# Attention's transposes and the previous step's products with the values in one burst per step, ordered by weight columns

## The chip, the cores and the metric

The kernel runs on one core of a Trainium2 chip. The metric is the device time of one execution in microseconds; three timed runs of the kernel before gave 1712.32, 1714.13 and 1714.29, so its median is 1714.13 us. The profile is one further execution of the same program, which took 1711.05 us.

## What is computed

One decoder block on 1024 tokens of width 1024 in float32: a pre-norm and one wide projection, then dilated sliding-window attention (24 heads in three groups) beside a causal convolution module, a gated merge, and a feed-forward part. The change touches the attention only. Of the reference, cut to what matters:

```python
qb = to_sub(q, 0).reshape(B, dilation, nb, BLOCK, H, Dh)       # queries, 128 a block
kb, vb = band(k), band(v)                                       # their keys and values
s = jnp.einsum('brnqhd,brnkhd->brnhqk', qb, kb) * (Dh ** -0.5) + bias
s = jnp.where(valid[:, None], s, NEG_INF)
lse = jax.nn.logsumexp(s, axis=-1)
p = jnp.exp(s - lse[..., None])
o = jnp.einsum('brnhqk,brnkhd->brnqhd', p, vb)
...
alpha = jax.nn.softmax(jnp.stack(lses, axis=0), axis=0)
o = jnp.einsum('gbsh,gbshd->bshd', alpha, jnp.stack(outs, axis=0))
```

## The kernel before, in words

Nearly all of the kernel is matrix products on TensorE. Every float32 operand is held as a rounded part "hi" and a rest "lo", and a product is three matmuls (hi by hi, hi by lo, lo by hi).

**Where attention lies.** Its work is not a stage of its own. `attention` (line 974) is a generator, and `beat` (line 139) advances it: each matmul of the loops that call `beat` adds RATE to a credit, and for each whole credit the generator runs to its next `yield`. Two loops carry it. The first is the projection of the values, `v` (lines 948, 950 and 952: 128x256 matmuls, called V matmuls below), at RV = 0.42. The second is the products of the convolution's output projection, `unit` (lines 305, 307 and 309: 128x512), at RU = 0.8. The emission order is the execution order: each engine takes its instructions one after the other, and an instruction that waits for another engine holds up what stands behind it on its own.

**One step.** There are 96 block-and-head-pair units in 12 stacks of 8 (group g, head pair hp, query block u) and 101 steps, because step s works on several units at once:

- `att_s` for unit s: four score matmuls (line 1049; 128 or 256 columns), two reductions on VectorE (line 1052) which add the bias and take the row's extremum. `att_e` for unit s-1: two exponentials on ScalarE with their accumulator reads (line 1062). Then a `yield`.
- `att_t` for unit s-4 (LT = 4): two to four 128x128 transposes through the identity (line 1087) into one PSUM bank. ScalarE copies the bank to hi (line 1094), VectorE makes lo from the bank and hi (line 1095). Then a `yield`.
- `att_p` for unit s-5 (LP = 5): the products with the values (line 1122), whose weights are 66 columns of the values and whose moving operand is hi or lo. In groups 0 and 1 there are three with 256 moving columns (called wide below), then three or six with 128 (slim); in group 2 six slim ones. After each of the first two triples there is a `yield`. For every second unit VectorE then copies the result out (line 1142, two copies).

So a step has four yields, and at 0.42 a yield is followed by two or three V matmuls; a step spans 9.5 of them. hi, lo, the scores' tiles and the bias tiles come from one ring of 11 half-size buffers (`half`). Loads of queries, keys and values are issued from SP's queue at the step's start, their doubling (lines 886, 887) and the splitting of the values (lines 917, 918, 922) go to POOL and ScalarE, and POOL's queue also issues the store of a finished stack (line 1149).

**Other work between.** Splits of weights for coming products (lines 188, 189), splits of the convolution's activations (lines 1242, 1243), and the merge of the three groups (lines 1170 to 1188; its one transpose is line 1183) are issued between the matmuls by `tick`.

Of the kernel before, what the change touches and what calls it, by code (L numbers as in the profile page):

```python
# [10 lines left out]
F32R = mybir.dt.float32r  # L11
AF = mybir.ActivationFunctionType
OP = mybir.AluOpType
# [16 lines left out]
ROOT = 1 / 32  # L30
LN_EPS = 1e-5

RV, RU = 0.42, 0.8


LD, PC = 2, (18, 20, 26)
# [22 lines left out]
def f(ap):  # L59
    return ap.bitcast(F32)  # L60


class Build:
# [909 lines left out]

    def attention(self):

        live, s, total = {}, 0, 96
        order = [(g, 2 * hg + i) for hg in range(2) for g in range(3) for i in range(2)]
        nxt, cur, u, x, V = self.stacks(*order.pop(0)), None, 8, None, None
        for i in range(5):
            self.stack_load(nxt)  # L980
        second = self.stacks(*order.pop(0))

        def there():
            return nxt[1] // 2 * 3 + nxt[0] < self.vn

        while s < total + self.LP:
            if s < total:
                if x is None and nxt and there():
                    x = self.values(*nxt[:2])
                if u == 8:  # L990
                    while self.normed < 9 or x is None:
                        if second and second[5] < min(5, self.normed - 4):
                            self.stack_load(second)
                        if x is None and there():
                            x = self.values(*nxt[:2])
                        yield 0
                    if cur is None:
                        self.double(nxt, 0)
                        self.double(nxt, 1)
                    cur, u, nxt, V = nxt, 0, None, []  # L1000
# [12 lines left out]
                if u in (6, 7) and nxt:  # L1013
                    self.double(nxt, u - 6)
                if u == 8:
                    cur[2] = cur[3] = V = None
                if u == 1:
                    if second:
                        nxt, second = second, None
                    elif order:  # L1020
                        nxt = self.stacks(*order.pop(0))
                if nxt and nxt[5] < 5:
                    self.stack_load(nxt)
            if 0 <= s - 1 < total:
                self.att_e(live[s - 1])
            yield 0
            if 0 <= s - self.LT < total:
                self.att_t(live, s - self.LT)
                yield 0
            if 0 <= s - self.LP < total:  # L1030
                yield from self.att_p(live, s - self.LP)
            s += 1

    def att_s(self, a, p, V, u):
# [41 lines left out]
    def att_t(self, live, k):  # L1076


        nc = self.nc
        a, b, hh = live[k & ~1], live[k | 1], k & 1  # L1080
        u = a["u"]
        items = [(a, u), (b, u), (a, u - 1), (b, u + 1)]
        items = [(x, x["blocks"].index(kb)) for x, kb in items if kb in x["blocks"]]
        ps = self.bank("t")
        for j, (x, i) in enumerate(items):
            c = hh * 256 + i * 128
            nc.tensor.transpose(ps[:, j * 128:(j + 1) * 128], x["sp"][:, c:c + 128], self.ident)  # L1087
        x = None
        if hh:
            a["sp"] = b["sp"] = None  # L1090
        n = len(items) * 128
        items = None
        hi, lo = self.half(F32R), self.half(F32R)
        nc.scalar.copy(hi[:, :n], ps[:, :n])
        nc.vector.tensor_tensor(lo[:, :n], ps[:, :n], f(hi[:, :n]), op=OP.subtract)
        a["pt", hh] = hi, lo

    def att_p(self, live, k):


        nc = self.nc
        a, b, hh = live[k & ~1], live[k | 1], k & 1
        g, hp, u = a["g"], a["hp"], a["u"]
        if hh == 0:
            a["o"] = self.bank("o")
        ps = a["o"]
        hi, lo = a.pop(("pt", hh))

        if g == 2:
            todo = [(u, 0, 128, 0), (u + 1, 128, 128, 128)]  # L1110
        else:
            n = 256 + 128 * (len(a["blocks"]) > 1)
            todo = [(u, 0, 256, 0)] + [(u - 1, 256, 128, 0)] * (n > 256) + [(u + 1, n, 128, 128)]
        for j, (kb, x, n, q) in enumerate(todo):
            kb = self.place(g, kb)
            v, w = a["V"][kb // 4]
            c = (kb % 4) * 256 + hh * 128
            vh = v[:, c:c + 66]
            vl = v[:, c + 64:c + 130] if c < 896 else w
            o = ps[0:66, hh * 256 + q:hh * 256 + q + n]  # L1120
            for i, (y, z) in enumerate(((vh, hi), (vl, hi), (vh, lo))):
                nc.tensor.matmul(o, y, z[:, x:x + n], start=i == 0 and j == 0, stop=i == 2 and j == len(todo) - 1,  # L1122
                                 skip_group_check=True)
            if j < 2:
                yield 0
        hi = lo = v = w = vh = vl = y = z = None
        if hh == 0:
            return
        if u == 0:
            self.O = self.ring()  # L1130

        O = self.O
        e = (8, 2, 128)[g]
        if g == 0:
            d = O.rearrange("p (c m) -> p m c", c=8)[:, u * 16:u * 16 + 32]
        elif g == 1:
            d = O.rearrange("p (e c m) -> p c m e", e=2, c=4)[:, u // 2]
        else:
            d = O[:, u * 128:u * 128 + 256].rearrange("p (c m) -> p c m", c=2)
        for h in range(2):  # L1140
            x = ps[0:64, h * 256:(h + 1) * 256]
            nc.vector.tensor_copy(d[h * 64:(h + 1) * 64], x.rearrange("p (a e) -> p a e", e=e))
        a["o"] = ps = d = x = O = None
        del live[k - 1], live[k]
        if u == 6:

            kept = g == 2 and hp > 1
            if not kept:
                self.later(1, lambda x=self.O: nc.gpsimd.dma_start(self.d_att[g, hp], x))
            if g == 2:  # L1150
                self.merges.append(self.bg(self.merge(hp, a["p"][4], self.O if kept else None)))
            self.O = None
# [882 lines left out]
```

## Time and profile before

| what | value |
|---|---|
| median of three runs | 1714.13 us |
| the profiled execution | 1711.05 us |
| span of its instructions | 1709.1 us |
| TensorE clock granted | 0.999 of full |
| first score matmul to last product with values | 614.9 to 862.7 us |
| of these, beside the V matmuls | to 793 us |
| products with values (line 1122) | 648, of them 192 wide |
| transposes (line 1087) | 280 |
| score matmuls (line 1049) | 384 |

The profile names instructions by engine and source line: PE is TensorE's matmuls, PEld its weight loads, DVE is VectorE, ACT is ScalarE, POOL is GpSimd. Matmuls overlap: each row's duration is latency too, so what a matmul costs is read from the distance between the starts of consecutive rows, not from its own duration. A row of the timeline that ends in "x3" is three instructions in a run, its time from the first start to the last end.

### The profile page before, as it was taken

To read this page: it belongs to the slowest core of one execution; us is meant where nothing else is said; L and a number is where in the kernel's file an instruction comes from. 1 tells how busy PE (TensorE), PEld (TensorE's weight loads), DVE (VectorE), ACT (ScalarE), POOL (GpSimd) and SP (SyncE) were. 2 spreads that over 40 slices of the span, in tenths; PEclk is the share of its full clock that TensorE was granted. 3 is DMA by queue.
4 is the path that set the end of the run, shared out by engine and by line. 5 is a ranking of instruction groups with operands and counts; after the bars stand their busy time and mean duration, and the time that the engine had idled before them with its cause. 6 is when DMAs were issued, how large, how long until landed. Compare 5 with 4: busy or idle time off the path is not lost.

```text
span 1709.1 us, 24547 instructions
## 1 busy us (share of the span) xinstructions
PE 1692.4 (99%) x8758; PEld 1437.4 (84%) x8758; DVE 1251.2 (73%) x2214; ACT 790.1 (46%) x1550; POOL 474.5 (28%) x383
## 2 busy tenths in 40 slices
PE   8999999999999999999999999999999999999998
PEld 7788888888888999999878888888888888888886
DVE  6789988888998667677885855775566556677686
ACT  6344344434444576677722436633333333354463
POOL 0017777887886124544300210000000000000000
PEclk9999999999999999999999999999999999999999
DMA  4352433455668887878998722123222322494234
GB/s 166 103 185 87 148 124 129 155 195 174 173 166 204 249 261 211 233 200 238 296 275 285 265 74 99 68 99 124 93 92 105 118 93 92 145 375 146 100 135 154
DMA packets 162422, 283.43 MB, mean 166 GB/s; under 512 B 47249, under 2 KB 78796, under 8 KB 162300
## 3 DMA queue, kind: packets, MB, share of 16 engines
q1 hardware_dynamic: 160204, 275.98, 50.8%
q0 software_dynamic: 1808, 5.61, 0.9%
q8 instruction: 69, 1.13, 0.3%
q14 instruction: 53, 0.43, 0.1%
q10 hardware_dynamic: 288, 0.27, 0.0%
HBM read 191.10 MB, written 95.42 MB: 168 GB/s over the span
## 4 chain that ended last, share of the span: by engine, by line
PE 95%; ACT 1%; issue 1%; DVE 1%; POOL 1%; DMA 1%; SPq 0%; DVEq 0%; ACTq 0%; POOLq 0%
PE p L321 16%; PE p L323 16%; PE p L322 16%; PE p L1919 12%; PE p L1648 5%; PE p L305 5%; PE p L307 5%; PE p L309 5%; PE p L1122 3%; PE p L948 2%; PE p L950 2%; PE p L952 2%; PE p L1049 2%; PE p L556 2%; PE p L1087 2%
## 5 line engine op out<-in xcount | busy, mean ns | idle before, releaser
L321 PE MATMUL p<-b,b 128*128 128x512 f32 x1204 | 468.6, 389 | 0.3 <-ACT c L340 0.3
L323 PE MATMUL p<-b,b 128*128 128x512 f32 x1204 | 468.4, 389 | 0.0
L322 PE MATMUL p<-b,b 128*128 128x512 f32 x1204 | 468.4, 389 | 0.0
L321 PEld LDWEIGHTS p<-b,b 128*128 128x128 f32 x1204 | 226.0, 188 | 47.8 <-ACT c L340 0.7
L322 PEld LDWEIGHTS p<-b,b 128*128 128x128 f32 x1204 | 226.0, 188 | 47.1
L323 PEld LDWEIGHTS p<-b,b 128*128 128x128 f32 x1204 | 226.0, 188 | 47.0
L1919 PE MATMUL p<-b,b 128*128 128x512 f32 x924 | 209.6, 389 | 0.0
L1919 PEld LDWEIGHTS p<-b,b 128*128 128x128 f32 x924 | 173.4, 188 | 36.0
L686 DVE SCALAR_TENSOR_TENSOR p<-b,par,p 128x511 f32<-128x511 f32 (+14 forms) x232 | 163.5, 739 | 0.0
L305 PE MATMUL p<-b,b 128*128 128x512 f32 x368 | 146.7, 399 | 1.3 <-ACT b L1242 1.2
L307 PE MATMUL p<-b,b 128*128 128x512 f32 x368 | 145.6, 396 | 0.0
L309 PE MATMUL p<-b,b 128*128 128x512 f32 x368 | 145.6, 396 | 0.0
L195 ACT CAST b<-d 128x1024 fp32r<-128x1024 f32 x86 | 90.4, 1051 | 105.1 <-POOL d L216 55.1
L196 POOL TENSOR_TENSOR b<-d,b 128x1024 fp32r<-128x1024 f32 x44 | 106.8, 2428 | 79.8 <-ACT b L195 72.4
L196 DVE TENSOR_TENSOR b<-d,b 128x1024 fp32r<-128x1024 f32 x42 | 51.3, 1222 | 101.0 <-ACT b L195 101.0
L948 PE MATMUL p<-b,b 128*128 128x256 f32 x384 | 112.8, 294 | 0.0
L952 PE MATMUL p<-b,b 128*128 128x256 f32 x384 | 112.2, 292 | 0.0
L950 PE MATMUL p<-b,b 128*128 128x256 f32 x384 | 112.2, 292 | 0.0
L1243 DVE TENSOR_TENSOR b<-b,b 128x512 fp32r<-128x512 f32 x133 | 91.7, 693 | 22.0 <-ACT b L1242 20.2
L1242 ACT CAST b<-b 128x512 fp32r<-128x512 f32 x133 | 82.1, 619 | 46.8 <-PE p L1919 18.1
L1648 PE MATMUL p<-b,b 128*128 128x512 f32 x384 | 89.4, 391 | 0.0
L195 ACT CAST b<-b 128x1024 fp32r<-128x1024 f32 x47 | 49.4, 1052 | 80.8 <-POOL b L223 37.2
(234 smaller groups left out, 3035.3 us busy)
## 6 DMA issues: line engine op xcount, KB each, us to landing
b<-w_in SPq DMA_DIRECT2D x30, 512.0 KB, 4.9
dk<-c SPq DMA_DIRECT2D x48, 256.0 KB, 2.9
dq<-c SPq DMA_DIRECT2D x48, 256.0 KB, 3.5
b<-dq SPq DMA_DIRECT2D x48, 256.0 KB, 4.3
b<-dk SPq DMA_DIRECT2D x48, 256.0 KB, 8.1
b<-w_fi SPq DMA_DIRECT2D x24, 512.0 KB, 4.8
d<-w_in SPq DMA_DIRECT2D x23, 512.0 KB, 4.8
dqS<-c SPq DMA_DIRECT2D x44, 256.0 KB, 2.2
```

Of the source, the lines that this page charges most:

```text
L196: self.wsplit.tensor_tensor(lo, x, f(hi), op=OP.subtract)
L305: nc.tensor.matmul(ps, hi[:, s], a, start=kt == 0, stop=False)
L307: nc.tensor.matmul(ps, hi[:, s], b, start=False, stop=False)
L309: nc.tensor.matmul(ps, lo[:, s], a, start=False, stop=kt == nk - 1)
L321: nc.tensor.matmul(ps, hi[:, s], a, start=first and kt == 0, stop=False, skip_group_check=True)
L322: nc.tensor.matmul(ps, hi[:, s], b, start=False, stop=False, skip_group_check=True)
L323: nc.tensor.matmul(ps, lo[:, s], a, start=False, stop=kt == 3, skip_group_check=True)
L686: nc.vector.scalar_tensor_tensor(A[i][:, j:], src[i][:, :H - j], w[i], A[i][:, j:], op0=OP.mult, op1=OP.add)
L948: nc.tensor.matmul(o, a, hi[:, s], start=kt == 0, stop=False)
L950: nc.tensor.matmul(o, a, lo[:, s], start=False, stop=False)
L1648: nc.tensor.matmul(banks[tt][nh], st, wt[:, nh * H:(nh + 1) * H], start=bool(kt == 0 and a), stop=bool(kt == KT - 1 and b))
L1919: nc.tensor.matmul(acc[t], x, y, start=first and e == 0, stop=last and e == 2, skip_group_check=True)
```

## The change

The transposes of unit s-4 and the products of unit s-5 are no longer issued by `att_t` and `att_p`: these return lists, and `attention` issues both lists as one burst. The lists are merged so: after each transpose come a share of the slim products (not after the first transpose, if there are wide ones) and a share of the wide ones. What followed the transposes (hi, lo) and the products (the copies out, now `att_o`) follows the burst. A step then has two yields in place of four, one after the scores and exponentials and one after the burst, and RV and RU are halved, so that a step spans 9.5 V matmuls as before. Steps 0 to 3, which have neither transposes nor products, have one yield as before, at the halved rate.

```diff
-RV, RU = 0.42, 0.8
+RV, RU = 0.21, 0.4
...
             yield 0
-            if 0 <= s - self.LT < total:
-                self.att_t(live, s - self.LT)
+
+            t, ts = self.att_t(live, s - self.LT) if 0 <= s - self.LT < total else ([], None)
+            p, ps = self.att_p(live, s - self.LP) if 0 <= s - self.LP < total else ([], None)
+            wide, slim = [m for m in p if m[2] == 256], [m for m in p if m[2] < 256]
+            todo, n = [], len(t)
+            for i in range(n):
+                todo.append(t[i])
+                if i or not wide:
+                    c = -(-len(slim) // (n - i))
+                    todo += slim[:c]
+                    slim = slim[c:]
+                c = -(-len(wide) // (n - i))
+                todo += wide[:c]
+                wide = wide[c:]
+            todo += wide + slim
...
+            for m in todo:
+                if len(m) == 2:
+                    nc.tensor.transpose(*m, self.ident)
+                else:
+                    (o, y), z, _ = m
+                    nc.tensor.matmul(o, y, z, start=first, stop=m is last, skip_group_check=True)
+                    first = False
...
+            if ts:
+                ts()
+            if ps:
+                ps()
+            ts = ps = None
+            if s >= self.LT:
                 yield 0
-            if 0 <= s - self.LP < total:
-                yield from self.att_p(live, s - self.LP)
             s += 1
...
-            nc.tensor.transpose(ps[:, j * 128:(j + 1) * 128], x["sp"][:, c:c + 128], self.ident)
...
+            todo.append((ps[:, j * 128:(j + 1) * 128], x["sp"][:, c:c + 128]))
         n = len(items) * 128
...
+        def then():
+            if hh:
+                a["sp"] = b["sp"] = None
+            hi, lo = self.half(F32R), self.half(F32R)
+            nc.scalar.copy(hi[:, :n], ps[:, :n])
+            nc.vector.tensor_tensor(lo[:, :n], ps[:, :n], f(hi[:, :n]), op=OP.subtract)
+            a["pt", hh] = hi, lo
+
+        return todo, then
...
-            for i, (y, z) in enumerate(((vh, hi), (vl, hi), (vh, lo))):
-                nc.tensor.matmul(o, y, z[:, x:x + n], start=i == 0 and j == 0, stop=i == 2 and j == len(todo) - 1,
-                                 skip_group_check=True)
-            if j < 2:
-                yield 0
...
+            ops += [((o, y), z[:, x:x + n], n) for y, z in ((vh, hi), (vl, hi), (vh, lo))]
         if hh == 0:
-            return
+            return ops, None
+        return ops, lambda: self.att_o(live, k, ps)
```

How the order moves, at the three places on which the prediction rests. In these rows `ident` is the identity that the transposes stream, `c` a half-size buffer (the scores' tile behind `ident`, else hi or lo), `b` a full-size buffer (weights and values) and `p` a PSUM bank.

The first place is TensorE in a step of group 1 beside the V matmuls. Before (line 1087 transposes, line 1122 products):

```order
L1087 MATMUL p_6662<-ident,c_6478 128x128 x2
L950 MATMUL p_6548<-b_5485,b_611 128x256
L952 MATMUL p_6548<-b_5484,b_634 128x256
L1122 MATMUL p_6672<-c_6621,b_6565 66x256 x2
L1122 MATMUL p_6672<-c_6622,b_6565 66x256
L948 MATMUL p_6548<-b_5484,b_625 128x256
L950 MATMUL p_6548<-b_5485,b_625 128x256
L952 MATMUL p_6548<-b_5484,b_658 128x256
L1122 MATMUL p_6672<-c_6621,b_6607 66x128 x2
L1122 MATMUL p_6672<-c_6622,b_6607 66x128
L948 MATMUL p_6548<-b_5484,b_645 128x256
```

And with the change (its line 1049 transposes, 1052 products):

```order
L952 MATMUL p_6701<-b_6489,b_743 128x256
L1049 MATMUL p_6758<-ident,c_6541 128x128
L1052 MATMUL p_6759<-c_6731,b_6582 66x256
L1049 MATMUL p_6758<-ident,c_6579 128x128
L1052 MATMUL p_6759<-c_6731,b_6626 66x128 x2
L1052 MATMUL p_6759<-c_6731,b_6582 66x256
L1049 MATMUL p_6758<-ident,c_6579 128x128
L1052 MATMUL p_6759<-c_6732,b_6626 66x128
L1052 MATMUL p_6759<-c_6732,b_6582 66x256
L948 MATMUL p_6701<-b_6489,b_731 128x256
```

The V matmuls between the pieces have moved out of the burst, and what stands ahead of the next V matmul is now a wide product, where it was a slim one.

The second place is TensorE in a step of group 2, where all products are slim. Before:

```order
L1122 MATMUL p_7568<-c_7520,b_7255 66x128 x2
L1122 MATMUL p_7568<-c_7521,b_7255 66x128
L948 MATMUL p_7375<-b_6542,b_784 128x256
L950 MATMUL p_7375<-b_6543,b_784 128x256
L1122 MATMUL p_7568<-c_7520,b_7255 66x128 x2
L1122 MATMUL p_7568<-c_7521,b_7255 66x128
L952 MATMUL p_7375<-b_6542,b_806 128x256
```

And with the change:

```order
L1049 MATMUL p_7579<-ident,c_7363 128x128
L1052 MATMUL p_7580<-c_7547,b_7276 66x128 x2
L1052 MATMUL p_7580<-c_7548,b_7276 66x128
L1049 MATMUL p_7579<-ident,c_7407 128x128
L1052 MATMUL p_7580<-c_7547,b_7276 66x128 x2
L1052 MATMUL p_7580<-c_7548,b_7276 66x128
L950 MATMUL p_7533<-b_7329,b_709 128x256
```

Of two places where a V matmul follows a slim product one is left; the other triple is followed by a transpose.

Over the whole attention, a slim product is followed by a V matmul 83 times before and 40 times now, by a 128x512 matmul of line 305, 307 or 309 45 times before and 16 now, and by a score matmul 24 times before and never now; a transpose is followed by a product never before and 277 times now.

The third place is VectorE, where the order within a step has stayed (reductions of the scores, lo, copies out), while what these wait for has moved on TensorE. With the change (its line 1082 is the reduction, 1126 lo, 1178 the copies, 189 a weight split):

```order
L1082 ISA c_6541,stat_6109<-p_6536,c_6295 128x128
L1082 ISA stat_6109 128x1
L1126 TENSOR_TENSOR c_6564<-p_6553,c_6563 128x384
L1178 COPY d_6404<-p_6517 64x128x2 x2
L1082 ISA c_6579,stat_6109<-p_6574,c_6295 128x256
L1082 ISA stat_6109 128x1
L189 TENSOR_TENSOR b_6490<-b_5947,b_6489 128x512
L1126 TENSOR_TENSOR c_6610<-p_6598,c_6609 128x384
```

The copies out of a pair stand between one lo and the next reduction, as before, and a weight split can stand ahead of a lo.

On POOL's queue the store of a stack's result has moved ahead of the first four of the next doubling copies, which it used to follow; on SP's queue loads have moved past one another by a few places, none by more than a step.

More of the change, by code (lines that the diff above doesn't have):

```diff
@@ L974, in attention @@
     def attention(self):
+        nc = self.nc
         live, s, total = {}, 0, 96
@@ L1026, in attention @@
             yield 0
-            if 0 <= s - self.LT < total:
-                self.att_t(live, s - self.LT)
+            t, ts = self.att_t(live, s - self.LT) if 0 <= s - self.LT < total else ([], None)
[12 more added lines that the diff above has]
+            todo += wide + slim
+            first, last = True, p[-1] if p else None
+            for m in todo:
+                if len(m) == 3:
+                    last = m
+            for m in todo:
+                if len(m) == 2:
[4 more added lines that the diff above has]
+                    first = False
+            t = p = todo = wide = slim = last = m = o = y = z = None
+            if ts:
[4 more added lines that the diff above has]
+            if s >= self.LT:
                 yield 0
-            if 0 <= s - self.LP < total:
-                yield from self.att_p(live, s - self.LP)
             s += 1
@@ L1084, in att_t @@
         ps = self.bank("t")
+        todo = []
         for j, (x, i) in enumerate(items):
             c = hh * 256 + i * 128
[L1087 to L1090, printed above, removed]
+            todo.append((ps[:, j * 128:(j + 1) * 128], x["sp"][:, c:c + 128]))
         n = len(items) * 128
[L1092 to L1096, printed above, removed]
+        def then():
[6 more added lines that the diff above has]
+        return todo, then
     def att_p(self, live, k):
@@ L1113, in att_p @@
             todo = [(u, 0, 256, 0)] + [(u - 1, 256, 128, 0)] * (n > 256) + [(u + 1, n, 128, 128)]
-        for j, (kb, x, n, q) in enumerate(todo):
+        ops = []
+        for kb, x, n, q in todo:
             kb = self.place(g, kb)
@@ L1120, in att_p, with att_o @@
             o = ps[0:66, hh * 256 + q:hh * 256 + q + n]
-            for i, (y, z) in enumerate(((vh, hi), (vl, hi), (vh, lo))):
-                nc.tensor.matmul(o, y, z[:, x:x + n], start=i == 0 and j == 0, stop=i == 2 and j == len(todo) - 1,
-                                 skip_group_check=True)
-            if j < 2:
-                yield 0
-        hi = lo = v = w = vh = vl = y = z = None
-        if hh == 0:
-            return
+            ops += [((o, y), z[:, x:x + n], n) for y, z in ((vh, hi), (vl, hi), (vh, lo))]
+        if hh == 0:
+            return ops, None
+        return ops, lambda: self.att_o(live, k, ps)
+    def att_o(self, live, k, ps):
+        nc = self.nc
+        a = live[k - 1]
+        g, hp, u = a["g"], a["hp"], a["u"]
         if u == 0:
@@ L1142, in att_p @@
             nc.vector.tensor_copy(d[h * 64:(h + 1) * 64], x.rearrange("p (a e) -> p a e", e=e))
-        a["o"] = ps = d = x = O = None
+        a["o"] = None
         del live[k - 1], live[k]
```

## The prediction

> **What bounds the kernel now.** I read the page first, then the busy times by stage, then the timeline of one step of attention.
>
> ```profile
> span 1709.1 us, 24547 instructions
> PE 1692.4 (99%) x8758; PEld 1437.4 (84%) x8758; DVE 1251.2 (73%) x2214; ACT 790.1 (46%) x1550; POOL 474.5 (28%) x383
> ...
> 614.00:660.00 46.00, 45.00 (x405) 44.35 (x405) 32.73 (x108) 34.12 (x105) 19.03 (x28) 1.00 0.81 245
> 793.00:830.00 37.00, 37.00 (x267) 31.67 (x266) 31.84 (x99) 29.64 (x94) 17.64 (x24) 1.00 0.96 268
> ```
>
> TensorE is never idle for long, also in the two stages shown (columns: stretch, length, then busy time of PE, PEld, DVE, ACT, POOL, clock, DMA share, GB/s): the first lies beside the V matmuls, the second beside the 128x512 matmuls. So attention costs what its matmuls take between starts. VectorE is the next engine, with 32.73 of 46 us in the one and 31.84 of 37 us in the other. The starts of TensorE's rows over one step of group 0 show where time is lost:
>
> ```profile
> 657.61 0.60 PE L1087 MATMUL p<-ident,c 128*128 128x128 f32 x4
> 657.96 0.36 PE L950 MATMUL p<-b,b 128*128 128x256 f32 x1
> 658.16 0.28 PE L952 MATMUL p<-b,b 128*128 128x256 f32 x1
> ...
> 658.40 0.51 PE L1122 MATMUL p<-c,b 128*66 128x256 f32 x3
> 658.75 0.28 PE L950 MATMUL p<-b,b 128*128 128x256 f32 x1
> 658.87 0.28 PE L952 MATMUL p<-b,b 128*128 128x256 f32 x1
> ...
> 659.45 0.34 PE L1122 MATMUL p<-c,b 128*66 128x128 f32 x3
> 659.63 0.69 PE L1049 MATMUL p<-b,b 128*128 128x256 f32 x4
> 660.15 0.28 PE L952 MATMUL p<-b,b 128*128 128x256 f32 x1
> 660.27 0.28 PE L948 MATMUL p<-b,b 128*128 128x256 f32 x1
> ...
> 661.19 0.51 PE L1122 MATMUL p<-c,b 128*66 128x256 f32 x3
> ...
> 661.78 0.34 PE L1122 MATMUL p<-c,b 128*66 128x128 f32 x3
> 661.96 0.33 PE L948 MATMUL p<-b,b 128*128 128x256 f32 x1
> 662.13 0.28 PE L950 MATMUL p<-b,b 128*128 128x256 f32 x1
> ```
>
> Three wide products take 658.40 to 658.75, 0.117 us each, and the V matmul behind them takes its usual 0.12 us (658.75 to 658.87). Three slim ones take 659.45 to 659.63, 0.06 us each, but the V matmul behind slim ones takes 0.17 us (661.96 to 662.13). The weight loads say why:
>
> ```profile
> L948 PEld LDWEIGHTS p<-b,b 128*128 128x128 f32 x225 | 42.8, 190 | 0.0
> L1122 PEld LDWEIGHTS p<-c,b 128*66 128x66 f32 x620 | 71.2, 137 | 5.8 <-POOL b L918 0.6 <-DVE c L1095 0.5
> L1087 PEld LDWEIGHTS p<-ident,c 128*128 128x128 f32 x280 | 34.1, 140 | 3.8
> L1087 PE MATMUL p<-ident,c 128*128 128x128 f32 x280 | 46.2, 272 | 0.0
> L1265 PE MATMUL p<-b,mean_col 128*128 128x512 f32 x4 | 1.9, 591 | 0.0
> ```
>
> The V matmul's load lasts 190 ns, the product's 137, 53 ns less; a load runs beside the matmul ahead of it, and 0.06 us of a slim product do not cover the longer one. Each step from a slim product to 128 columns of weights so loses 0.05 us.
>
> **Part by part.** *Slim products' successors.* Ahead of a V matmul such steps fall from 83 to 40: 43 x 0.05 = 2.15 us. Ahead of a 128x512 matmul they fall from 45 to 16, at 0.06 us by these rows (0.29 us behind slim products, then 0.23):
>
> ```profile
> 861.05 0.34 PE L1122 MATMUL p<-c,b 128*66 128x128 f32 x3
> 861.24 0.45 PE L307 MATMUL p<-b,b 128*128 128x512 f32 x1
> 861.53 0.40 PE L309 MATMUL p<-b,b 128*128 128x512 f32 x1
> 861.76 0.27 PE L1183 MATMUL p<-ident,mrg 128*48 128x128 f32 x1
> ```
>
> That is 29 x 0.06 = 1.74 us. Ahead of score matmuls they fall from 24 to none; no row isolates the price, the weights are 128 columns too, so 24 x 0.05 = 1.2 us. Together -5.1 us, bounded by the rounding of the rows at about -4 and -6.
>
> *The transposes.* Four start within 0.60 less the last one's 0.272 us, so 0.109 us apart. The order is worth more if this is their weight load, which a wide product would hide, and nothing if it is their streaming. The only other unrounded float32 matmuls are line 1265's:
>
> ```profile
> 554.15 1.88 PE L1265 MATMUL p<-b,mean_col 128*128 128x512 f32 x4
> ```
>
> They start (1.88 - 0.591) / 3 = 0.43 us apart for 512 columns, so 0.107 for 128, which is the transpose's 0.109. And the transpose's load of 140 ns is like that of 66 columns, not that of 128. I take streaming: a transpose costs 0.109 us wherever it stands, and slim products cover its load. The Trainium skill, "TensorE: Matmul & The Clock Gate", section "LDWEIGHTS (loading the stationary operand)", puts a load at columns / 1.2 ns, which by an estimate from that page is 107 ns for any 128 columns; the 140 against 190 ns speak against it for transposes.
>
> *Changes between kinds.* A transpose was followed by a product nowhere. From the first transpose to the second V matmul behind it (657.61 to 658.16) pass 0.55 us, four times 0.109 plus 0.117, so leaving costs nothing that two decimals show; at most 0.01 us for each of some 180 more changes, 1.8 us. V matmuls in longer runs take 0.12 us where one ahead of a product takes about the products' own 0.117: 135 more such pairs (376 before, 511 now) x 0.003. I take +0.4, between 0 and +1.8.
>
> *The start.* Two waits of the first steps come from a crowd on ScalarE and POOL:
>
> ```profile
> 620.07 0.75 PE L1049 MATMUL p<-b,b 128*128 128x256 f32 x4 [0.53 <-DVE stat L1052]
> 622.13 0.83 PE L1122 MATMUL p<-c,b 128*66 128x256 f32 x3 [0.40 <-POOL b L918]
> ```
>
> Steps 0 to 3 now last five V matmuls in place of two or three, so the crowd thins: -0.9 us, between 0 and -0.9.
>
> *Later operands.* This is what the burst costs. Today lo of the step shown is ready well ahead:
>
> ```profile
> 658.24 0.59 ACT L1094 CAST c<-p 128x512 fp32r<-128x512 f32 x1 [1.13 <-PE p L1087]
> ...
> 658.86 0.69 DVE L1095 TENSOR_TENSOR c<-p,c 128x512 fp32r<-128x512 f32 x1 [0.83 <-ACT c L1094]
> 659.83 1.23 DVE L1142 COPY d<-p 64x256 f32<-64x256 f32 x2 [0.28 <-PE p L1122]
> ```
>
> lo ends at 659.55 and the first product that reads it, the third of 661.19, starts at 661.42: 1.87 us to spare. In a burst of four transposes, three wide and six slim products (4 x 0.109 + 3 x 0.117 + 6 x 0.06 = 1.15 us) the last transpose starts at 0.92 and ends, with its 0.27, at 1.19; hi takes 0.03 + 0.59 and lo 0.03 + 0.69, so lo ends at 2.53. The step lasts 1.15 + 0.47 for the scores (the 0.52 of 659.63 to 660.15 less the stall) + 9.5 x 0.12 = 2.76 us, and the first use of lo stands behind three transposes, two wide and two slim products, 0.68 us into the next burst, at 3.44. 0.91 us are left. Behind lo on VectorE stand the copies out and the next reductions, for which the exponentials wait; ahead of it may stand a weight split:
>
> ```profile
> ACT c L1094 <- PE p L1087: 62.9, 73, 1.7
> DVE c L1095 <- ACT c L1094: 29.3, 46, 1.3
> PEld p L1122 <- DVE c L1095: 0.5, 2, 0.3
> L189 DVE TENSOR_TENSOR b<-b,b 128x512 fp32r<-128x512 f32 x20 | 14.7, 734 | 9.9 <-ACT b L188 9.5 <-DMA stat<-dst 0.2
> L1243 DVE TENSOR_TENSOR b<-b,b 128x512 fp32r<-128x512 f32 x16 | 11.6, 727 | 1.1 <-ACT b L1242 1.1
> ```
>
> ScalarE waits for the transposes in 73 of 96 cases and VectorE for hi in 46, so mostly both stand ready; one split of 0.73 us fits into 0.91, two overrun it by 0.55. With two such places in full that is 1.1 us; I take +1.1, from 0 up to the third rival's sum.
>
> *POOL.* The store that moves ahead of four doubling copies waits for the copies out; the doubled columns are read three steps (8 us) later, and POOL is busy 19.03 of 46 us. I cost it at nothing; without that cover it would be at most the 1.23 us of the copies per stack.
>
> The sum is -5.1 + 0.4 - 0.9 + 1.1 = -4.5 us: of the profiled execution's 1711.05 us, 1706.55. The median of the runs lies 3.08 us above that execution, so I forecast 1714.13 - 4.5 = 1709.6 us.
>
> **The rivals.** *Given back.* The start's waits stay (0 for -0.9) and lo is late at five or six places by 0.55 us, 3.0 us in all: -5.1 + 0.4 + 3.0 = -1.7, 1712.4 us. For it speaks that the margin halves, against it that products waited for lo only twice.
>
> *VectorE's queue sets the step.* Slower: the 20 and 16 splits of lines 189 and 1243 come two by two, 18 places. At half of them both stand ahead of lo (2 x 0.73 - 0.91 = 0.55 us), at half one stands there with the copies out (1.23 + 0.73 - 0.91 = 1.05 us): 9 x 0.55 + 9 x 1.05 = 14.4 us, less 5.6 us for the other terms gives +8.8, 1722.9 us. It decides from 9.0 / 18 = 0.5 us a place. For it speaks VectorE's 31.84 of 37 us beside the 128x512 matmuls; against it the 29.3 us in which it waits for hi.
>
> *Transposes bound by their loads.* Then 277 transposes that short loads follow cost 0.06 in place of 0.109 us, -13.6, and the 32 behind slim products stall by 0.05, +1.6: with the rest -16.5, 1697.6 us. The Trainium skill's rule on loads, named above, gives this outcome; the 0.43 us of line 1265 speak against it.
>
> **How the numbers follow.** The forecast has 48 in 100, giving back 30, the queue 17, the loads 5. A measurement here tells changes over 0.2%, 3.4 us, from none: faster is below 1710.7, slower above 1717.6 us. Of the forecast 45 lie below 1710.7, with 2 of giving back and the 5 of the loads: 0.52 faster. Of the queue 16 and of giving back 1 lie above: 0.17 slower, and 0.31 remain. The forecast's own range is 1707 to 1711.5 us (price of a stall, changes between kinds). The range of 1704 to 1720 takes in giving back and half of the queue's rival, and leaves out some 18.
>
> **What would show it.** Right: in the changed timeline the V matmul behind a wide product takes 0.12 us; a transpose between products keeps 0.109 us; waits of products for lo sum to some 1 us; the first steps wait less. Wrong: a transpose behind a wide product at 0.06 us (the loads), rows of products with 0.5 us and more of idle time ahead, released by VectorE or ScalarE, in most stacks (the queue), or a change between transpose and product that costs 0.01 us and more.

## The result, and the profile after

The changed kernel takes 1719.06 us in the median of seven runs, the kernel before 1712.32 us in seven beside it: the ratio is 1.0032, with a 95% interval of 1.0020 to 1.0045. The ratio weighs all runs of both kernels; the two medians alone lie 6.7 us apart. By the ratio the changed kernel is slower by some 5.5 us, where 4.5 us faster was forecast. The profiled execution took 1716.85 us with a span of 1714.7 us, 5.6 us over the span before.

The head of the page and the two stages that the prediction showed (stretch, length, busy time of PE, PEld, DVE, ACT, POOL, then clock, DMA share, GB/s), of the changed kernel:

```profile
span 1714.7 us, 24539 instructions
PE 1693.1 (99%) x8758; PEld 1440.5 (84%) x8758; DVE 1250.1 (73%) x2214; ACT 788.8 (46%) x1550; POOL 475.0 (28%) x383
...
614.00:660.00 46.00, 43.03 (x379) 42.80 (x377) 30.07 (x98) 30.64 (x94) 18.60 (x27) 0.96 0.84 245
793.00:830.00 37.00, 36.64 (x264) 32.39 (x263) 31.72 (x100) 29.68 (x93) 16.11 (x24) 1.00 0.92 271
```

In the first stage TensorE is now idle for 3.0 of 46 us, where it had 1.0 us, and its mean clock is 0.96. The burst itself does what it should. TensorE's timeline of one step of group 1 of the changed kernel (transposes line 1049, products 1052):

```profile
680.90 0.27 PE L1049 MATMUL p<-ident,c 128*128 128x128 f32 x1
680.92 0.36 PE L1052 MATMUL p<-c,b 128*66 128x256 f32 x1
681.12 0.27 PE L1049 MATMUL p<-ident,c 128*128 128x128 f32 x1
...
681.77 0.28 PE L948 MATMUL p<-b,b 128*128 128x256 f32 x1
681.89 0.28 PE L950 MATMUL p<-b,b 128*128 128x256 f32 x1
```

A transpose and a wide product take 0.22 us together (680.90 to 681.12), the sum of the 0.109 and 0.117 forecast, and the V matmul behind the burst, which ends on a wide product, takes 0.12 us. So the transposes behind V matmuls and wide products are bound by their streaming, and the stall behind slim products is gone there. What is new are waits. The groups of waits of the changed kernel between 612 and 875 us (who waits for whom: us in total, times, longest):

```profile
PE p L1052 <- ACT c L1125: 3.8, 2, 3.0
PE p L1052 <- DVE c L1126: 2.5, 2, 2.1
PE p L305 <- ACT b L1278: 1.5, 2, 0.9
PE p L307 <- DVE b L1279: 0.8, 2, 0.6
...
DVE c L1126 <- ACT c L1125: 54.7, 56, 4.3
...
ACT d L960 <- DMA datt<-d: 4.9, 1, 4.9
```

Of the two waits of 3.8 us for hi (line 1125) one is 3.0 us, and ScalarE waited once, for 4.9 us, for a DMA. They are one event. The timeline of the changed kernel shows the store of the first stack's result on POOL's queue, ScalarE, and TensorE:

```profile
645.23 0.57 POOL L1185 DMA_DIRECT2D datt<-d  x1 [2.21 <-DVE d L1178]
...
647.99 0.59 ACT L1125 CAST c<-p 128x512 fp32r<-128x512 f32 x1 [1.18 <-PE p L1049]
653.46 0.58 ACT L960 COPY d<-p 128x512 f32<-128x512 f32 x1 [4.88 <-DMA datt<-d]
...
654.93 0.57 ACT L1125 CAST c<-p 128x512 fp32r<-128x512 f32 x1
...
652.31 0.27 PE L1049 MATMUL p<-ident,c 128*128 128x128 f32 x1
655.55 0.34 PE L1052 MATMUL p<-c,b 128*66 128x256 f32 x1 [2.97 <-ACT c L1125]
...
657.71 0.42 PE L952 MATMUL p<-b,b 128*128 128x256 f32 x1
657.93 0.42 PE L948 MATMUL p<-b,b 128*128 128x256 f32 x1
```

Line 960 copies a finished bank of the V projection into a 128x1024 buffer of `ring`, of which there are three; attention's results go into the same three. The copy stands at the head of ScalarE's queue from 648.58 us, and the buffer that it gets is still read by the store issued at 645.23. ScalarE takes its work in order, so the hi behind the copy ends only at 655.50, and the first wide product of step 16, which reads it, waits 2.97 us. Then TensorE runs at half its clock: V matmuls start 0.22 us apart (657.71, 657.93) in place of 0.12. The same stretches of the changed kernel, and of the kernel before:

```profile
652.00:656.00 4.00, 1.03 (x9) 0.80 (x9) 0.47 (x1) 2.54 (x9) 0.00 (x0) 0.97 1.04 242
656.00:659.00 3.00, 3.00 (x19) 3.00 (x18) 1.61 (x7) 1.85 (x8) 0.93 (x1) 0.50 0.88 197
```

```profile
652.00:656.00 4.00, 4.00 (x39) 4.00 (x38) 2.83 (x10) 2.42 (x7) 0.59 (x1) 1.00 1.03 245
656.00:659.00 3.00, 3.00 (x31) 3.00 (x30) 1.49 (x8) 1.87 (x7) 0.00 (x0) 1.00 0.23 54
```

In the second stretch 19 matmuls run in place of 31. In the kernel before the same copy got the buffer of the same store, but came later:

```profile
644.88 0.57 POOL L1149 DMA_DIRECT2D datt<-d  x1
...
652.56 0.59 ACT L1094 CAST c<-p 128x512 fp32r<-128x512 f32 x1 [1.19 <-PE p L1087]
653.27 0.59 ACT L960 COPY d<-p 128x512 f32<-128x512 f32 x1
```

That store landed 8.3 us after its issue, at 653.2, just ahead of the copy at 653.27. The changed kernel has the copy ready 3.4 us behind the store's issue, not 8.4, because attention lags behind the V matmuls, which set the time of the copy: in steps 0 to 3 a yield still stands once a step, at the halved rate, and when step 16 begins 635 V matmuls have been issued in place of 619.

For comparing kernels I take from TensorE's trace each step's length less what its matmuls take when undisturbed (by their starts: V 0.118 us, 128x512 0.228, wide 0.117, slim 0.059, transpose 0.109, and the scores). Runs named here are described below. In us:

| steps | before | changed | align | slot | align_tfirst |
|---|---|---|---|---|---|
| 4 and 5 | 1.8 | 0.05 | 1.8 | 0.05 | 2.0 |
| 16 | 0.2 | 4.6 | 0.1 | 0.1 | 0.1 |
| 48 | 0.2 | 0.15 | 1.7 | 0.15 | 1.6 |
| 56 | 0.2 | 1.3 | 0.1 | 1.4 | 0.1 |
| 85 to 88 | 1.1 | 3.0 | 3.0 | 4.5 | 3.0 |
| 93 and 94 | 0.7 | 5.2 | 1.0 | 5.2 | 1.0 |
| all 95 | 14.2 | 23.1 | 16.0 | 19.9 | 13.5 |

And the mean of the quiet steps (those under 0.26 us) from step 8 on, in ns:

| group | before | changed | align | align_tfirst | slimlast | g2tail |
|---|---|---|---|---|---|---|
| 0 | 111 | 87 | 85 | 38 | 80 | 36 |
| 1 | 116 | 83 | 74 | 48 | 99 | 53 |
| 2 | 161 | 128 | 128 | 115 | 130 | 90 |

### The profile page after: what moved, and what is told of

The parts are those of the page before. It is cut to its first block, busy times and chain, and to the rows that moved or that the text cites. A ratio compares the mean times of both kernels' runs of the same rounds, so it can differ in the third digit from the quotient of the medians.

```text
span 1714.7 us, 24539 instructions
## 1 busy us (share of the span) xinstructions
PE 1693.1 (99%) x8758; PEld 1440.5 (84%) x8758; DVE 1250.1 (73%) x2214; ACT 788.8 (46%) x1550; POOL 475.0 (28%) x383
## 4 chain that ended last, share of the span: by engine, by line
PE 94%; DMA 2%; ACT 1%; POOL 1%; issue 1%; DVE 0%; DVEq 0%; SPq 0%; ACTq 0%; POOLq 0%
PE p L321 16%; PE p L322 16%; PE p L323 16%; PE p L1955 12%; PE p L1684 5%; PE p L307 5%; PE p L305 5%; PE p L309 5%; PE p L950 3%; PE p L948 3%; PE p L952 3%; PE p L1052 2%; PE p L556 2%; PE p L1079 2%; PE p L1049 1%; DMA datt<-d 1%
## 5 line engine op out<-in xcount | busy, mean ns | idle before, releaser
L321 PE MATMUL p<-b,b 128*128 128x512 f32 x1204 | 468.9, 389 | 0.3 <-ACT c L340 0.3
L323 PE MATMUL p<-b,b 128*128 128x512 f32 x1204 | 468.7, 389 | 0.0
L322 PE MATMUL p<-b,b 128*128 128x512 f32 x1204 | 468.7, 389 | 0.0
L1955 PE MATMUL p<-b,b 128*128 128x512 f32 x924 | 209.6, 389 | 0.0
L305 PE MATMUL p<-b,b 128*128 128x512 f32 x368 | 145.8, 396 | 1.5 <-ACT b L1278 1.5
L307 PE MATMUL p<-b,b 128*128 128x512 f32 x368 | 144.7, 393 | 0.8 <-DVE b L1279 0.8
L309 PE MATMUL p<-b,b 128*128 128x512 f32 x368 | 144.7, 393 | 0.0
L948 PE MATMUL p<-b,b 128*128 128x256 f32 x384 | 110.7, 288 | 0.0
L950 PE MATMUL p<-b,b 128*128 128x256 f32 x384 | 110.2, 287 | 0.0
L952 PE MATMUL p<-b,b 128*128 128x256 f32 x384 | 110.1, 287 | 0.0
L1052 PE MATMUL p<-c,b 128*66 128x128 f32 (+1 forms) x620 | 96.5, 280 | 6.2 <-ACT c L1125 3.8
L1126 DVE TENSOR_TENSOR c<-p,c 128x384 fp32r<-128x384 f32 (+2 forms) x96 | 52.4, 545 | 55.6 <-ACT c L1125 54.7
```

What stands on the lines that cost most here:

```text
L305: nc.tensor.matmul(ps, hi[:, s], a, start=kt == 0, stop=False)
L307: nc.tensor.matmul(ps, hi[:, s], b, start=False, stop=False)
L309: nc.tensor.matmul(ps, lo[:, s], a, start=False, stop=kt == nk - 1)
L321: nc.tensor.matmul(ps, hi[:, s], a, start=first and kt == 0, stop=False, skip_group_check=True)
L322: nc.tensor.matmul(ps, hi[:, s], b, start=False, stop=False, skip_group_check=True)
L323: nc.tensor.matmul(ps, lo[:, s], a, start=False, stop=kt == 3, skip_group_check=True)
```

## The experiments

Theory A: the loss is the lag, by the collision in step 16. Theory B: the burst leaves hi and lo too little time, so that anything that holds up ScalarE or VectorE stops TensorE. Ratios are to the kernel before, with 95% intervals.

**The lag taken out.** `align` is the changed kernel with:

```diff
-    fine, RATE, credit = None, RV, 0
+    fine, RATE, credit = None, 2 * RV, 0
...
+            if s == self.LT + 1:
+                self.RATE = RV
```

> The changed kernel, with attention's first five steps paced as before: the credit per matmul stays 0.42 until step 5 and is halved from there, so that attention no longer lags the V matmuls by about 14 of them. Theory A (the loss is that lag: a projection's copy on ScalarE meets a stack's store that has not yet freed its ring slot, and the clock falls behind the idle): the 4.9 us wait of ScalarE in step 16 is gone with the 4.5 us that it cost, and the kernel is within 2 us of the one before (ratio 0.999 to 1.001). Theory B (the burst halves the time that hi and lo have, and late operands stop TensorE wherever a queue is held up): other places than step 16 lose as much, and the kernel stays 4 to 6 us slower than before (ratio 1.0025 to 1.0035).

Measured: 1712.42 us, ratio 0.9996 (0.9988 to 1.0005). The copy comes at 654.08, 8.8 us after the store's issue at 645.28, and waits for nothing; step 16 loses 0.1 us. Theory A holds for the slowdown, but the kernel is not clearly faster than before either: most of the forecast gain is still missing.

**Transposes first, and both.** `tfirst` is the changed kernel with one line for the merging of the lists, `align_tfirst` has both edits:

```diff
+            todo = t + slim + wide
```

> The changed kernel with the burst in another order: all transposes, then the slim products, then the wide ones. hi and lo can start 0.4 to 0.7 us earlier, as much as stands behind the last transpose; the burst still ends on a wide product, the lag stays. Theory A: step 16 keeps its wait for the store (4.9 us on ScalarE) and most of its 4.5 us, the kernel stays 4 to 5.5 us slower than before (ratio 1.0023 to 1.0032). Theory B: the margin of lo nearly doubles, the waits of products for hi and lo between steps 50 and 96 (some 8 us by the excess over the ideal) shrink to 3 us or less, and the kernel is within 2 us of before (ratio 0.999 to 1.001).

> Both of these edits: early steps paced as before, and transposes first in the burst. If lag and late operands both cost, their gains add: 4.5 us from step 16 and some 4 us from the later steps off the 5.6 us by which the changed kernel is slower, so 2 to 4 us faster than before (ratio 0.9977 to 0.999), which is the gain of the weight loads that the prediction saw. Theory A alone: as the first of these runs, within 1 us. Theory B alone: as the second.

`tfirst` took 1715.34 us, ratio 1.0012 (1.0003 to 1.0021); `align_tfirst` 1708.98 us, ratio 0.9976 (0.9966 to 0.9986), faster than both kernels. But theory B's reason for it is not borne out: in the profile of `tfirst` products still wait 6.5 us for hi and lo besides the 2.5 us of step 16, not under 3. (That execution took 1717.99 us, 2.7 us over the median of its runs.) What was gained stands in the quiet steps, 47, 26 and 13 ns in groups 0, 1 and 2 between `align` and `align_tfirst`, 2.8 us over 32 steps each. TensorE's timeline of the burst of step 15 in `align_tfirst`:

```profile
649.03 0.60 PE L1041 MATMUL p<-ident,c 128*128 128x128 f32 x4
649.38 0.96 PE L1044 MATMUL p<-c,b 128*66 128x128 f32 x9
650.18 0.28 PE L950 MATMUL p<-b,b 128*128 128x256 f32 x1
650.30 0.28 PE L952 MATMUL p<-b,b 128*128 128x256 f32 x1
```

And the ends of the same burst in the changed kernel:

```profile
649.58 0.27 PE L1049 MATMUL p<-ident,c 128*128 128x128 f32 x1
...
650.54 0.36 PE L1052 MATMUL p<-c,b 128*66 128x128 f32 x2
650.74 0.33 PE L950 MATMUL p<-b,b 128*128 128x256 f32 x1
650.91 0.28 PE L952 MATMUL p<-b,b 128*128 128x256 f32 x1
```

Four transposes, nine products and the V matmul behind them take 1.27 us in the one and 1.33 us in the other: with four transposes the change's merging still ends on two slim products, and the V matmul takes 0.17 us. Over the attention slim products stand ahead of a V matmul 15 times with the new line, 40 times in the changed kernel. Nor does a transpose stand behind a slim product any more, as it does in each of the 32 steps of group 2 in the changed kernel, where it costs 0.025 us more than elsewhere.

**The lag alone.** `lag` is the kernel before with RATE at half of RV up to step 4.

> The kernel before with the lag alone: the credit per matmul is 0.21 up to step 4 and 0.42 from there, so attention starts as late as in the changed kernel, and its steps are the old ones with four yields. Theory A: the projection's copy meets the unfinished store in step 16 as in the changed kernel, ScalarE waits some 4 us, and the kernel is 2.5 to 4.5 us slower than before (ratio 1.0015 to 1.0026); the first steps' two waits are gone. Theory B: with lo's old margin of 1.87 us the lag costs nothing, ratio 0.9993 to 1.0007.

Measured: 1712.33 us, ratio 0.9991 (0.9981 to 1.0002). Theory A as I had put it is refuted: the copy comes at 648.78, as early as in the changed kernel, and does not wait for a store. The waits that the programs set ahead of the copy tell why (SW stands for POOL's queue, HW for SP's). The changed kernel:

```
L960 COPY d_6058<-p_5835 128x2x2x128 [waits DMAHW3_49,DMASW4_49,PE_49]
```

The kernel before with the lag:

```
L960 COPY d_6055<-p_5832 128x2x2x128 [waits DMAHW3_49,DMAHW2_49,PE_49]
```

With the old steps the copy stands just ahead of the second stack's first result in the order of the program, and gets another buffer. So here the lag costs only together with the buffer that the copy is given.

**That buffer alone.** Two runs test it in the changed kernel. `ring4` has NRING = 4, with NSLOT = 41 for 42. `slot` issues two stores of the projection two ticks sooner, ahead of three loads in SP's queue, which changes the order in which buffers come free:

```diff
-                self.later(5, lambda i=i, x=x: out(i, x))
+                self.later(3 if (g, hg, i) == (2, 0, 6) else 5, lambda i=i, x=x: out(i, x))
```

> The changed kernel with four ring buffers in place of three (and 41 full-size buffers in place of 42, to make room). The projection's copy in step 16 then gets a slot that no store of attention still reads. If that wait is what the lag costs: ScalarE's 4.9 us wait and step 16's 4.5 us are gone, and the kernel is 0 to 2 us slower than before (ratio 1.0000 to 1.0012). If the lag costs through the last ten steps, which run beside the 128x512 matmuls (7.6 us over the ideal in steps 86 to 94 of the changed kernel's profile, 3.0 in the run that had the first steps paced as before): 4.5 to 6 us slower (ratio 1.0026 to 1.0035).

> The changed kernel, lag and order of the burst as they are, but the last two stores of the projection ahead of attention's second stack are issued two ticks sooner, ahead of three loads on SP's queue. By that the slot which they free comes up first, and the projection's copy of step 16 takes it, in place of the slot that the store of the first stack's result still reads. If that slot's wait is what step 16 costs: ScalarE's 4.9 us and step 16's 4.5 us over the ideal go, and the kernel is 0.5 to 2 us slower than before (ratio 1.0003 to 1.0012). If the lag or the burst costs in other ways (ScalarE late for other reasons there, or the last ten steps alone): 4.5 us and more slower (ratio 1.0026 or above).

`ring4` took 1753.03 us, ratio 1.0228 (1.0208 to 1.0248): the missing full-size buffer costs 33 us before attention begins, so its time decides nothing; step 16 lost 0.1 us. `slot` took 1714.78 us, ratio 1.0001 (0.9990 to 1.0012), so 0.0031 of the changed kernel's 0.0032 is gone. ScalarE's timeline and two stretches of `slot`:

```profile
648.12 0.59 ACT L1125 CAST c<-p 128x512 fp32r<-128x512 f32 x1 [1.18 <-PE p L1049]
648.60 0.59 ACT L960 COPY d<-p 128x512 f32<-128x512 f32 x1
649.08 0.52 ACT L1092 ACTIVATE c<-c,stat 128x256 f32<-128x256 f32 x1
```

```profile
652.00:656.00 4.00, 4.00 (x40) 4.00 (x39) 2.36 (x8) 1.89 (x8) 0.92 (x1) 1.00 1.00 327
656.00:659.00 3.00, 3.00 (x32) 3.00 (x31) 2.00 (x10) 1.57 (x5) 0.00 (x0) 1.00 0.20 59
```

The lag is there (the copy at 648.60), the burst is there, and neither step 16's wait nor the low clock behind it is. So it is shown that the slowdown against the kernel before comes from this one buffer. Why the kernel is then no faster than before is another question, taken up below.

**The last ten steps.** The lagging kernels also lose more in steps 85 to 94 of their profiles. `catchup` takes the lag out again in steps 40 to 42, `latelag` puts it into `align` in steps 60 to 62:

```diff
+            if s in (40, 43):
+                self.RATE = {40: 2 * RV, 43: RV}[s]
```

```diff
+            if s in (5, 60, 63):
+                self.RATE = {5: RV, 60: 2 / 3 * RV, 63: RV}[s]
```

> The changed kernel, lagging as it does up to step 40, where three steps run at twice the pace, so that attention is back in step with the V matmuls long before the 128x512 matmuls begin. Step 16's wait stays. If that alone is what the lag costs, the kernel stays 4.5 to 6 us slower than before (ratio 1.0026 to 1.0035); if the last ten steps cost as well, some 4 us of the 7.6 over the ideal there go, and it is 1 to 3 us slower (ratio 1.0006 to 1.0018).

> The changed kernel with its first steps paced as before (the first of the runs, ratio 0.9996), but in steps 60 to 62 attention runs at two thirds of the pace, so that it lags by 14 V matmuls from there on, as much as in the changed kernel. Step 16 stays clear. If the lag costs in the last ten steps by itself, beside the 128x512 matmuls: 3 to 5 us slower than the run without it (ratio 1.0013 to 1.0025). If those steps lose by chance of the interleaving, lag or no lag: within 1.5 us of it (ratio 0.9987 to 1.0005).

`catchup` stays at 1720.13 us, ratio 1.0034 (1.0022 to 1.0045), and its profile still loses 8 us in steps 84 to 94, without the lag; `latelag` is at 1712.7 us, 0.9986 (0.9976 to 0.9995), no slower than `align`, with the lag. So the lag by itself costs nothing there. How these steps lose anything is shown by the queues of ScalarE and VectorE in step 86 of the changed kernel, and by TensorE:

```profile
833.03 0.37 ACT L1125 CAST c<-p 128x256 fp32r<-128x256 f32 x1
...
834.76 1.00 DVE L189 TENSOR_TENSOR b<-b,b 128x512 fp32r<-128x512 f32 x1 [0.53 <-DMA dgc<-b]
835.68 1.09 DVE L1279 TENSOR_TENSOR b<-b,b 128x512 fp32r<-128x512 f32 x1
836.70 0.41 DVE L1126 TENSOR_TENSOR c<-p,c 128x256 fp32r<-128x256 f32 x1
...
837.16 0.28 PE L1052 MATMUL p<-c,b 128*66 128x128 f32 x1 [2.11 <-DVE c L1126]
```

hi is ready at 833.40, but on VectorE a split that waits 0.53 us for a DMA, and a second split behind it, of some 1 us each, hold up lo until 836.70, and TensorE stops for 2.11 us. This is theory B's event, and it is real, but how much it costs differs from kernel to kernel: steps 85 to 88 lose from 1.1 us (before) to 8.0 us (`tfirst`) in the profiles.

**Catching up early.** `early` has `tfirst`'s order and the lag, which steps 5 to 10 take out again.

> Transposes first, with the lag of steps 0 to 4 kept, and caught up in steps 5 to 10, which run at four thirds of the pace, before the projection's copy of step 16 comes. The waits of steps 4 and 5 (2.0 us over the ideal in the profile of the run that had both edits, 0.05 in those that lag) should go and step 16 stay clear: 1.5 to 2 us faster than that run, 5.6 to 6.2 us faster than before (ratio 0.9964 to 0.9967). If the faster steps only move the crowd on ScalarE and POOL, or step 16's wait returns: ratio 0.9976 or above.

Measured: 1713.02 us, ratio 0.9991 (0.9978 to 1.0004). A miss: steps 4 and 5 lose 0.1 us and step 16 nothing, as hoped, but steps 84 to 94 lose 8 us. VectorE waited there twice for DMAs:

```profile
829.56 0.75 DVE L1614 SCALAR_TENSOR_TENSOR b<-p,par,b 128x512 f32<-128x512 f32 x1 [2.02 <-DMA b<-dgc]
...
835.50 0.29 DVE L1074 CUSTOM_DVE_ANT_0 c<-p,c 128x128 f32<-128x128 f32 x1 [2.02 <-DMA c<-rep]
```

**What the end of a burst is worth.** `slimlast` is `align_tfirst` with the wide products ahead of the slim ones.

> Early steps paced as before and transposes first, as in the run that had both, but the wide products ahead of the slim ones, so that bursts end on a slim product: a slim product is followed by a V matmul 66 times in place of 15 and by a 128x512 matmul 29 times in place of 16. By the prediction's prices that is 51 x 0.05 + 13 x 0.06 = 3.3 us, so 0.5 to 1.5 us faster than before where the other was 4.1 faster (ratio 0.9990 to 0.9998). If the end on a wide product is not what gains, it stays at 0.9976.

Measured: 1711.95 us, ratio 0.9986 (0.9977 to 0.9995). The quiet steps of groups 0 and 1 are 42 and 51 ns longer than in `align_tfirst`, one stall a step at the prediction's 0.05 us, 3.0 us over 64 steps; the ratios differ by 0.0010, 1.7 us, and the two intervals overlap.

**Two more orders.** `lolast` and `g2tail` change the one line of `align_tfirst`; `g2tail` has the second piece too:

```diff
+            todo = t + [m for c in (0, 1) for q in (slim, wide) for i, m in enumerate(q) if (i % 3 == 2) == c]
...
+            if not wide:
+                todo = todo[len(t):] + t
```

> Early steps paced as before and transposes first, and in each kind of products those that read lo behind those that read hi: all transposes, slim by hi, wide by hi, slim by lo, wide by lo. lo is first read 0.24 to 0.35 us later in the burst. Theory B: the waits of products for lo that were left (0.6 us in the profile of the run without this) go, and it is up to 1 us faster than that run (ratio 0.9970 to 0.9976). If a change from slim to wide and back costs on TensorE, 64 steps with two more of them lose: 0.9980 and above.

> As the run with lo's products last, and in group 2, where all products are slim, the transposes behind the products, so that no burst there ends on a slim product: 32 stalls of 0.045 us go, 1.4 us faster than that run (ratio 0.0008 below it), against hi and lo 0.36 us later in group 2. If a V matmul stalls behind a transpose as well, or lo gets late: no faster than that run.

`lolast` took 1708.86 us, ratio 0.9971 (0.9960 to 0.9982), `g2tail` 1709.41 us, ratio 0.9971 (0.9962 to 0.9981). Both beat the kernel before and the changed one; among themselves and against `align_tfirst` the intervals do not tell them apart. In group 2 the quiet step of `g2tail` is 16 ns shorter than that of `lolast` (106 ns), where 45 ns were expected. TensorE's trace shows most of what is missing: the first transpose, which now stands behind a slim product, takes 0.132 us to the next start in place of 0.108, so the stall has in good part moved from the V matmul to the transpose.

## Why the prediction was wrong, point by point

*POOL, "I cost it at nothing", and The start, -0.9.* This is the main step that failed. I asked of the moved store only who reads the doubled columns behind it, and not who needs the buffer that it reads; and I took the longer first steps as a gain alone. The store is issued at nearly the same time (645.23, before 644.88), but the lag moved the projection's copy from behind that store's landing to 4.9 us ahead of it. Step 16's 4.4 us more than before are most of the slowdown: with another buffer the ratio is 1.0001 in place of 1.0032. That is a little over half of the 10 us between forecast and result; the rest is the gain that does not come. As to what it did forecast, the start was right in kind and too small: steps 4 and 5 lost 1.8 us before and 0.05 us after.

*Later operands, +1.1.* The event was foreseen, and its size is the second thing that failed. The margin of 0.91 us was weighed against splits of 0.73 us on VectorE alone. What overran it were waits of the in-order queues for DMAs: 4.88 us on ScalarE in step 16, 0.53 us on VectorE with two splits of some 1 us behind it in step 86, and 2.02 us on VectorE in `early`. The prediction weighed none of these waits for DMAs, nor the half clock that came behind some of the idles. (Its bound for this term, "up to the third rival's sum", can only mean the 14.4 us of VectorE's queue, which is its second rival.) That the range of 1704 to 1720 us holds the 1719.06 us is luck: it was that wide for other rivals, not for a copy that waits for a store.

*Slim products' successors, -5.1, and changes between kinds, +0.4.* Of the first, mechanism and price were right: 0.12 us behind a wide product, 42 to 51 ns a stall in `slimlast`. The second was mis-sized: the quiet steps of the changed kernel are 24, 33 and 33 ns shorter, 32 x 0.090 = 2.9 us where both terms together had 4.7. `align`, which has the same bursts and whose clock did not fall, shows what makes up the difference when each matmul's distance to the next start is set against its undisturbed figure. V, 128x512 and score matmuls behind slim products lose 2.9 us where they lost 8.5 us before, so that the first term gains 5.6 us. Against it 0.8 us are lost in 32 transposes that stand behind slim products, 1.1 us more in slim and wide products behind slim ones (4 ns each, where slim behind slim lost 1.4 ns before), and 1.0 us more in the longer runs of V and 128x512 matmuls. The sign of being wrong, a change between transpose and product at 0.01 us and more, did come for these 32.

*Transposes.* Streaming it is: 0.109 us behind V matmuls, wide products and transposes, so the rival of the loads is out. But "slim products cover its load" was wrong: behind a slim product a transpose costs 0.134 us in the changed kernel.

*VectorE's queue.* Not what bounds the kernel: VectorE waited 54.7 us for hi, 29.3 before. It hits single steps, not most stacks.

*The gain that does not come.* With its collision removed the changed kernel equals the one before instead of gaining 4.5 us. The same account of distances, from the first score matmul to the last product with the values, in us over the undisturbed figures (a distance that is over by more than 0.11 us counts as a wait):

| | before | changed | align | slot |
|---|---|---|---|---|
| at full clock, no wait | 12.9 | 9.5 | 9.9 | 9.3 |
| waits | 4.0 | 11.0 | 9.1 | 8.0 |
| at half clock | 0 | 3.3 | 0 | 3.6 |

So the order of the burst gives 3.0 to 3.6 us in all three, and waits and the half clock take it back. The kernel before has a further wait of 1.2 us behind its last product, at the merge's transpose, which the others do not have; with it the sums differ as the profiled spans do, to 0.4 us. In the profile of `slot` two groups of waits are each followed by a low clock: 2.07 us for lo in step 86, and 2.3 us in step 93 for the splits of the convolution's activations.

```profile
832.63 0.28 PE L1052 MATMUL p<-c,b 128*66 128x128 f32 x1 [2.07 <-DVE c L1126]
...
833.58:836.99 3.41, 3.41 (x17) 3.01 (x16) 2.91 (x9) 2.01 (x8) 1.69 (x3) 0.50 1.02 410
854.06:857.47 3.41, 3.41 (x15) 2.92 (x16) 1.26 (x5) 0.00 (x0) 0.00 (x0) 0.50 0.97 318
```

*What stays open.* These are single executions, and the one of the kernel before was a good one, 1711.05 us where its runs beside the experiments had medians of 1713.3 to 1714.0. For the low clock of `slot` all its runs speak: the mean granted clock is 0.997 or less in 9 of 12, and in 7 of the 35 runs of the kernel before beside them. Which of the waits come in which run, and why they hit these steps, is not shown.

## What to carry to other kernels

When a change moves one stream of work against another, list for every buffer that the two share who frees it and when, DMA landings included: here a store cost nothing until the next user of its buffer came early. An operand's margin has to be held against the longest wait in the queue of the engine that makes it, and not against the work in that queue alone. An order of a burst is best tried without shifting the start: with the transposes first and the old pace in the first steps, the bursts were worth 0.0024 to 0.0029 of the time.

## What the hardware showed

Behind one idle of 2.97 us TensorE's granted clock was 0.50 for 3.41 us, so that the wait cost about half as much again: step 16 lost 4.6 us. The Trainium skill, "TensorE: Matmul & The Clock Gate", section "Part 1: The HAM clock gate (the "warmup" mystery)", has the clock fall to half after an idle window of about 3.4 us; the half agrees, the 2.97 us are below its window. Nor was a single long idle needed: in the changed kernel TensorE was idle for 2.3 us of one stretch, in four waits of at most 0.86 us, and the clock of the next was 0.57:

```profile
850.00:857.00 7.00, 4.69 (x30) 3.38 (x29) 3.90 (x14) 3.99 (x16) 1.49 (x2) 1.00 1.05 229
857.00:861.00 4.00, 4.00 (x18) 3.47 (x19) 1.41 (x6) 0.37 (x1) 0.00 (x0) 0.57 1.02 280
```

The kernel before, idle for 1.3 us of the first of these stretches in one wait, kept its clock:

```profile
850.00:857.00 7.00, 5.71 (x38) 4.35 (x37) 5.21 (x18) 3.10 (x13) 0.00 (x0) 1.00 1.05 238
857.00:861.00 4.00, 4.00 (x31) 3.21 (x30) 2.21 (x7) 0.97 (x3) 0.00 (x0) 1.00 1.05 235
```

Nor does the length of an idle decide alone in these traces: the wait of 2.11 us in step 86 left the changed kernel's clock at 1.00, and the like wait of 2.07 us in `slot` was followed by 3.41 us at 0.50, by which step 87 lost 1.7 us there and 0.2 us in the changed kernel.

The ten stores of a stack's result, 512 KB each, took between 2.9 and 9.2 us to land in the changed kernel, so that here a buffer's time of release could not be read from the store's issue.
